# Making the recurrence's elementwise tiles in the projections, in pieces of 128 tokens, with own weight splits and an inverse in two pipeline stages

## The chip, the cores and the metric

The kernel runs on one core of a Trainium2 chip. The metric is the device time of an execution in microseconds; a kernel's time is the median of its timed executions. Engines are named as in the profile; SP here only issues DMAs.

## What is computed

One inference step of a two-layer decoder with 1024 channels, in fp32, for a prompt of 1024 tokens and eight samples of 8 tokens each. Layer 0 mixes by a convolution module, layer 1 by RWKV-7 time mixing; each layer then has cross-attention over 256 memory tokens and an MLP of width 4096. The change lies in layer 1's mixer:

```python
r = xr @ p['rw_w_r'][ri]; k = xk @ p['rw_w_k'][ri]; v = xv @ p['rw_w_v'][ri]
w_pre = p['rw_w0'][ri] + jnp.tanh(xw @ p['rw_w1'][ri]) @ p['rw_w2'][ri]
decay = jnp.exp(-jnp.exp(-jax.nn.softplus(-w_pre) - 0.5))
a = jax.nn.sigmoid(p['rw_a0'][ri] + (xa @ p['rw_a1'][ri]) @ p['rw_a2'][ri])
g = jax.nn.sigmoid(xg @ p['rw_g1'][ri]) @ p['rw_g2'][ri]
kk = k * p['rw_k_k'][ri]                       # then divided by its norm, per head
k = k * (1 + (a - 1) * p['rw_k_a'][ri])
y, s = wkv7_scan(rh, decay, kh, vh, -kk, kk * ah, s0)   # state 64x64 per head, token by token
y = standardize(y, LNX_EPS) * p['rw_lnx_g'][ri] + p['rw_lnx_b'][ri]
bonus = jnp.sum(rh * kh * p['rw_r_k'][ri], axis=-1, keepdims=True) * vh
out = ((y + bonus) * g) @ p['rw_w_o'][ri]
```

## The kernel before

**Two streams.** Stream A carries the first 512 prompt tokens, stream B the other 512 with the 64 sample tokens (576 columns). Each goes through convolution, attention 0, MLP 0, projections, recurrence, output product, attention 1 and MLP 1. The streams are generators; `pace` takes the next step of the one whose summed costs are lower, and a scheduler that works with a simulated timeline then orders each engine's instructions, the recurrence with 1000 instructions of priority. B's recurrence needs A's final state, so it waits for "scan0"; B's MLP 1 runs alone at the end. On-chip memory is given to pools in stacks, A's from the left and B's from the right, and a pool that takes over memory waits for the tiles that held it.

**Split products.** Large products run as three fp32r matmuls on the high and low halves of both operands (`prod`, L142 to L144). `split` makes the halves: ACT copies the high one (L96), DVE subtracts (L97). A weight tile is 128x1024. For the 24 weight tiles of r, k and v, A also writes the low half to DRAM (`put`, tile low) and B loads it from there instead of subtracting.

**Projections** (`projections`). Mixed tokens are made for r, k and v in turn (`mix`), and `project` multiplies them with eight weight tiles, m = 0 to 7, for two token tiles of 256 (A) or 288 (B). Beside the products run sides, one step for each product: `hidden` makes the low-rank inner products (L810), `lora` the outer ones (L856) with Tanh, Sigmoid or a copy behind. Every result goes to DRAM in six slots for each m (scr). The low-rank product for a ran last, after all of `project`.

**Recurrence** (`scan`). A chunk is 64 tokens with all channels, 128 x 512 elements for each quantity; A has 8 chunks, B the samples as one chunk and 8 more. `prep` loads a chunk's r, k, decay input, a and v from scr, makes on DVE, ACT and POOL the key kk, the running sum of the decay (a scan instruction, L1171), its two exponentials, and from them the tiles ar and bk that PE reads, the bonus factor and the head norms; then PE forms the products within the chunk (L1224) and DVE masks them (Aak, Aq). `invert` inverts the chunk's triangular blocks, first in blocks of 16 on DVE, then in blocks of 32 with PE. `rest` does the step on the state (`step`) and `finish` (norm per head, weight, bias, bonus and gate on POOL). `together` interleaves the steps of three chunks: rest of chunk n-2, inverse of n-1, prep of n.

What sets the order around the change: each engine takes its instructions as the scheduler left them, so an instruction that waits holds those behind it; SP does so with the DMAs that it issues.

## Time and profile before

| | us |
| --- | --- |
| median of three timed executions (3832.77 to 3837.16) | 3834.26 |
| the profiled execution | 3837.42 |
| its span, first to last instruction | 3835.7 |
| PE busy in the span (94%) | 3623.9 |
| DVE busy (61%) | 2351.6 |
| ACT busy (42%) | 1610.0 |
| POOL busy (17%) | 660.7 |

How to read it: matmuls are pipelined, so PE's busy time holds work at half clock and waits inside the pipe too; two rows of products at full clock give what one costs.  The first instruction of A's recurrence on PE starts near 1745 us and its last near 2121; B's lie between 2391 and 2862.

### The profile page before, as it was taken

To read this page: it belongs to the slowest core of one execution; us is meant where nothing else is said; L and a number is where in the kernel's file an instruction comes from. 1 tells how busy PE (TensorE), PEld (TensorE's weight loads), DVE (VectorE), ACT (ScalarE), POOL (GpSimd) and SP (SyncE) were. 2 spreads that over 40 slices of the span, in tenths; PEclk is the share of its full clock that TensorE was granted. 3 is DMA by queue.
4 is the path that set the end of the run, shared out by engine and by line. 5 is a ranking of instruction groups with operands and counts; after the bars stand their busy time and mean duration, and the time that the engine had idled before them with its cause. 6 is when DMAs were issued, how large, how long until landed. Compare 5 with 4: busy or idle time off the path is not lost.

```text
span 3835.7 us, 75763 instructions
## 1 busy us (share of the span) xinstructions
PE 3623.9 (94%) x30906; PEld 3369.6 (88%) x30906; DVE 2351.6 (61%) x4479; ACT 1610.0 (42%) x3190; POOL 660.7 (17%) x704
## 2 busy tenths in 40 slices
PE   8989979999999999999979998879999999989998
PEld 7767769999999999998768898758799999989998
DVE  7889974646545554437896444778955546553334
ACT  3223253435433354544555654444543435332222
POOL 0010031114201100002332000243330025101110
PEclk9999989999999999999979998889899999989998
DMA  6414223335422344544333784432233336322222
GB/s 226 132 53 129 80 67 106 102 114 170 153 90 83 126 151 152 159 138 112 85 88 109 232 254 146 111 93 70 54 113 120 114 120 197 121 72 83 83 83 64
DMA packets 333004, 456.03 MB, mean 119 GB/s; under 512 B 155248, under 2 KB 247664, under 8 KB 332656
## 3 DMA queue, kind: packets, MB, share of 16 engines
q1 hardware_dynamic: 305008, 424.43, 36.4%
q10 hardware_dynamic: 27648, 26.75, 2.0%
q8 instruction: 243, 3.98, 0.4%
q14 instruction: 105, 0.86, 0.1%
HBM read 369.11 MB, written 73.49 MB: 115 GB/s over the span
## 4 chain that ended last, share of the span: by engine, by line
PE 77%; DVE 11%; ACT 4%; DMA 4%; issue 2%; POOL 1%; SPq 1%; ACTq 0%; DVEq 0%; POOLq 0%
PE B_d L142 11%; PE B_d L144 11%; PE B_d L143 11%; PE A_d L142 10%; PE A_d L143 9%; PE A_d L144 9%; PE A_d L362 3%; PE B_d L362 2%; DMA scr<-t_st 1%; SPq L1151 1%; PE A_hd L810 1%; PE A_d L442 1%; PE B_sa L608 1%; DVE wt L97 1%; PE B_sa L610 1%
## 5 line engine op out<-in xcount | busy, mean ns | idle before, releaser
L97 DVE TENSOR_TENSOR wt<-raw,wt 128x1024 fp32r<-128x1024 f32 x447 | 567.3, 1272 | 476.9 <-ACT wt L96 473.0
L96 ACT CAST wt<-raw 128x1024 fp32r<-128x1024 f32 x488 | 508.5, 1047 | 502.2 <-PE B_d L144 268.6
L142 PE MATMUL B_d<-hAB,wt 128*128 128x288 f32 (+1 forms) x2240 | 673.6, 303 | 15.4 <-ACT hAB L96 6.3
L143 PE MATMUL B_d<-hBB,wt 128*128 128x288 f32 (+1 forms) x2240 | 668.5, 299 | 1.2 <-DVE hBB L97 1.1
L144 PE MATMUL B_d<-hAB,wt 128*128 128x288 f32 (+1 forms) x2240 | 666.2, 298 | 0.3 <-DVE wt L97 0.3
L142 PE MATMUL A_d<-hAA,wt 128*128 128x256 f32 x2240 | 639.1, 288 | 15.0 <-ACT hAA L96 13.6
L143 PE MATMUL A_d<-hBA,wt 128*128 128x256 f32 x2240 | 642.4, 288 | 3.4 <-DVE hBA L97 3.4
L144 PE MATMUL A_d<-hAA,wt 128*128 128x256 f32 x2240 | 632.8, 285 | 2.5 <-POOL wt L97 2.2
L142 PEld LDWEIGHTS A_d<-hAA,wt 128*128 128x128 f32 x2240 | 429.0, 192 | 25.1 <-ACT hAA L96 16.8
L142 PEld LDWEIGHTS B_d<-hAB,wt 128*128 128x128 f32 x2240 | 425.4, 191 | 24.5 <-ACT hAB L96 7.5
L143 PEld LDWEIGHTS A_d<-hBA,wt 128*128 128x128 f32 x2240 | 430.2, 192 | 14.3 <-DVE hBA L97 5.6
L144 PEld LDWEIGHTS A_d<-hAA,wt 128*128 128x128 f32 x2240 | 428.6, 192 | 7.3 <-POOL wt L97 2.6
L143 PEld LDWEIGHTS B_d<-hBB,wt 128*128 128x128 f32 x2240 | 427.2, 191 | 6.5 <-DVE hBB L97 3.7
L711 POOL TENSOR_TENSOR t_sg<-t_ev 128x256 f32<-128x256 f32 (+1 forms) x256 | 185.5, 725 | 1418.2 <-ACT t_ev L709 1329.3
L144 PEld LDWEIGHTS B_d<-hAB,wt 128*128 128x128 f32 x2240 | 426.1, 190 | 2.3 <-issue 0.7
L142 PE MATMUL B_d<-u,wt 128*128 128x288 f32 x1024 | 307.1, 301 | 0.0
L144 PE MATMUL B_d<-u,wt 128*128 128x288 f32 x1024 | 303.3, 299 | 0.0
L143 PE MATMUL B_d<-u,wt 128*128 128x288 f32 x1024 | 303.3, 298 | 0.0
L143 PE MATMUL A_d<-u,wt 128*128 128x256 f32 x1024 | 288.2, 282 | 0.0
L144 PE MATMUL A_d<-u,wt 128*128 128x256 f32 x1024 | 288.2, 282 | 0.0
L142 PE MATMUL A_d<-u,wt 128*128 128x256 f32 x1024 | 287.4, 282 | 0.0
L97 DVE TENSOR_TENSOR u<-t_sg,u 128x256 fp32r<-128x256 f32 (+1 forms) x256 | 130.4, 510 | 149.9 <-ACT u L96 149.6
(401 smaller groups left out, 7068.8 us busy)
## 6 DMA issues: line engine op xcount, KB each, us to landing
raw<-in_mlp_up_dram SPq DMA_DIRECT2D x128, 512.0 KB, 3.6
raw<-in_mlp_dn_dram SPq DMA_DIRECT2D x128, 512.0 KB, 3.6
raw<-in_rw_w_dram SPq DMA_DIRECT2D x64, 512.0 KB, 4.2
ld<-scr SPq DMA_DIRECT2D x136, 128.0 KB, 3.2
wf<-in_w_in_dram SPq DMA_DIRECT2D x32, 512.0 KB, 4.0
raw<-in_xa_w_q_dram SPq DMA_DIRECT2D x32, 512.0 KB, 3.6
raw<-in_xa_w_o_dram SPq DMA_DIRECT2D x32, 512.0 KB, 3.6
raw<-in_ck_dram SPq DMA_DIRECT2D x32, 512.0 KB, 3.6
```

The lines of the kernel that those rows point to most:

```text
L96: self.nc.scalar.copy(hi, src)
L97: (engine or self.nc.vector).tensor_tensor(lo, src, hi.bitcast(F32), SUB)
L142: self.nc.tensor.matmul(out, lhsT=wh, rhs=mh, start=(i == 0), stop=False)
L143: self.nc.tensor.matmul(out, lhsT=wh, rhs=ml, start=False, stop=False)
L144: self.nc.tensor.matmul(out, lhsT=wl, rhs=mh, start=False, stop=(i == last))
L362: nc.tensor.matmul(ps[:, :n], lhsT=wt[:, 0, k * P:k * P + P], rhs=h[:, k, t0:t0 + n], start=(k == 0), stop=(k == NC8 - 1))
L442: nc.tensor.matmul(ps[hs], lhsT=dg[:, q, h], rhs=two[h][:, 2 * q:2 * q + 512], start=(q == 0), stop=(q == pairs - 1))
L608: nc.tensor.matmul(out[:, h2], lhsT=wt.rearrange("p i t -> p (i t)"), rhs=moving[:, 0], start=start, stop=stop)
L610: nc.tensor.matmul(out[:64, h2], lhsT=wt[:, 0], rhs=moving[:, 1], start=False, stop=False)
L711: nc.gpsimd.tensor_mul(sg[:, :n], r[:, :n], r[:, :n])
L810: nc.tensor.matmul(ps[:, :n], lhsT=w1[:, m:m + P], rhs=hc[:, :n], start=(c == 0), stop=(c == NC8 - 1))
L1151: nc.sync.dma_start(out=dst[..., m * 64:m * 64 + 64], in_=scr[part][m][:, slots, t0:t0 + 64])
```

## The change

**Elementwise tiles.** A new generator `stage(m, c0)` loads the six slots of one m for a piece of 128 tokens (64 for the samples), makes in place r times the decay, kk times the decay, the two tiles of bk, the gated bonus with the bias, and the gate with the weight, and stores the six to a new DRAM tensor, tls. Its tiles kk, t1 and ones (the exponentials) have one buffer, ld has three for A and two for B. There are 32 pieces for A and 40 for B; `project` steps through the pieces of m behind the last product of v for that m. Head norms go to a small tile sums, chunk-end decays to ends. The low-rank product for a becomes a side of `project(2)`, its hidden one of `project(0)`. In the recurrence `prep` loads four of the six slots straight into what PE reads (ld, two buffers), and `finish` loads the other two and runs three POOL instructions where there were five.

**Weight splits.** Both streams split their own weights: `put` and low are gone.

**Inverse.** In two stages: `blocks16` follows `prep` of the same chunk once at is there (`begun`), and `blocks32` runs a round later beside the next chunk's `begun`. dgz and td get two buffers.

```diff
-        if share is not None and self.part:
-            self.nc.scalar.copy(wt[:, 0], raw)
-            self.nc.sync.dma_start(out=wt[:, 1].bitcast(F32), in_=share)
-            return wt
...
-    low = [[dram.tile([P, 1024], F32, name=f"low{i}_{m}") for m in range(NC8)] for i in range(3)]
+
+    tls = [[dram.tile([P, 6, n], F32, name=f"tls{i}_{m}") for m in range(NC8)] for i, (_, n, _) in enumerate(PARTS)]
+
+    sums = [const.tile([P, NC8, n], F32, name=f"sums{i}") for i, n in enumerate((8, 9))]
+    ends = [const.tile([P, NC8, n], F32, name=f"ends{i}") for i, n in enumerate((8, 16))]
...
-        weights = s.weights([(a["rw_w"][i, m], 1024, P, None, None, low[i][m]) for i in range(3) for m in range(NC8)])
...
-        one, lh = (hp.tile([P, np_], F32R, name=f"l{n}") for n in "wh")
+        weights = s.weights([(a["rw_w"][i, m], 1024, P) for i in range(3) for m in range(NC8)])
+
+        lw, la, lh = (hp.tile([P, np_], F32R, name=f"l{n}") for n in "wah")
...
-        hid = {"w": one, "a": one, "h": lh}
+        hid = {"w": lw, "a": la, "h": lh}
...
+        half, pieces = 128, (0, 2, 4, 6, 8)[:4 + part]
+        rst = hp.tile([P, half], F32, name="rst")
+
+        ones = hp.tile([P, half // 64 * 65], F32, name="ones")
+        nc.gpsimd.memset(ones, 1.0)
...
+        less = hp.tile([P, NC8], F32, name="less")
...
+        def stage(m, c0):
+
+            n, l, e, rs, at = (64, DSEQ, tail, tail_rst, slice(8, 16)) if c0 == 8 else (half, 64, ones, rst, slice(c0, c0 + 2))
+            ts = slice(64 * c0, 64 * c0 + n)
+            ld = hp.tile([P, 6, half], F32, tag="ld", name="ld", bufs=3 - part)
+            nc.sync.dma_start(out=ld[:, :, :n], in_=scr[part][m][:, :, ts])
+            w, r, ag, k, v, g = (ld[:, i, :n] for i in range(6))
+            kk, t1 = (hp.tile([P, half], F32, tag=x, name=x)[:, :n] for x in ("kk", "t1"))
+            e = by(e, l + 1)
+            nc.scalar.activation(kk, k, AF.Copy, scale=col("k_k", m))
+            nc.scalar.activation(t1, k, AF.Square, scale=col("k_k", m))
+            ps = s.bank()
+            for i in range(n // 64):
+                for hs in (slice(0, 64), slice(64, P)):
+                    nc.tensor.matmul(ps[hs, i:i + 1], lhsT=t1[hs, 64 * i:64 * i + 64], rhs=bones[hs, hs][:, :1],
+                                     start=True, stop=True)
+            nc.vector.tensor_scalar_max(sums[part][:, m, c0:c0 + n // 64], ps[:, :n // 64], L2_MIN)
+
+            nc.vector.tensor_tensor_scan(out=w, data0=rs, data1=w, initial=0.0, op0=MUL, op1=ADD)
+            nc.scalar.activation(e[:, :, 1:], by(w, l), AF.Exp, scale=-DECAY)
+            nc.scalar.activation(w, w, AF.Exp, scale=DECAY)
+            yield .2
+            nc.scalar.activation(t1, ag, AF.Identity, scale=col("k_a", m), bias=less[:, m:m + 1])
+            nc.vector.scalar_tensor_tensor(out=ag, in0=kk, scalar=-1.0, in1=ag, op0=MUL, op1=MUL)
+            nc.vector.scalar_tensor_tensor(out=t1, in0=t1, scalar=1.0, in1=k, op0=ADD, op1=MUL)
+            nc.gpsimd.tensor_tensor(ag, ag, w, MUL)
+            nc.vector.tensor_tensor(k, t1, w, MUL)
+            nc.vector.scalar_tensor_tensor(out=t1, in0=r, scalar=col("r_k", m), in1=t1, op0=MUL, op1=MUL)
+            nc.gpsimd.tensor_copy(ends[part][:, m, at], e[:, :, l])
+            nc.gpsimd.tensor_tensor(by(r, l), by(r, l), e[:, :, 1:], MUL)
+            nc.vector.tensor_tensor(by(w, l), by(kk, l), e[:, :, :l], MUL)
+            yield .2
+            ps = s.bank()
+            nc.tensor.matmul(ps[:, :n], lhsT=bones, rhs=t1, start=True, stop=True)
+            nc.vector.tensor_tensor(v, v, ps[:, :n], MUL)
+
+            nc.vector.scalar_tensor_tensor(out=v, in0=v, scalar=col("lnx_b", m), in1=g, op0=ADD, op1=MUL)
+            nc.scalar.activation(g, g, AF.Copy, scale=col("lnx_g", m))
+            yield .2
+            nc.sync.dma_start(out=tls[part][m][:, :, ts], in_=ld[:, :, :n])
+
+        def staged():
+
+            for m in range(NC8):
+                yield 0
+                for c0 in pieces:
+                    yield from stage(m, c0)
...
-                        store(t, m, (slot + 1) % 3, t0, n)
+                        store(t, m, (1, 3, 4)[slot], t0, n)
                         yield cost(n)
                         for side in sides:
                             yield next(side, 0)
+                    if slot == 2 and tt == tiles[-1]:
+                        for _ in range(1 + 3 * len(pieces)):
+                            yield next(tiles_of, 0)
                     if m0 == 6 and after is not None:
...
-        yield from project(0, 2, hidden(1, "w", [AF.Tanh]))
-        yield from project(1, 3, hidden(5, "gh", [AF.Sigmoid, AF.Sigmoid]), lora("w", 3))
-        yield from project(2, None, hidden(4, "a", [AF.Copy]), lora("gh", 5))
-        s.put()
-        yield from lora("a", 4)
+        tiles_of = staged()
+        yield from project(0, 2, hidden(1, "w", [AF.Tanh]), hidden(4, "a", [AF.Copy]))
+        yield from project(1, 3, hidden(5, "gh", [AF.Sigmoid, AF.Sigmoid]), lora("w", 0))
+        yield from project(2, None, lora("a", 2), lora("gh", 5))
+        yield from tiles_of
...
-BUF = dict(w=5, bon=2, at=2, ar=2, Aq=2, UV=2, AV=2, BK=2, v=2, pcs=3)
+BUF = dict(w=5, ld=2, at=2, Aq=2, UV=2, AV=2, BK=2, v=2, pcs=3, td=2)
...
-    E65 = filled([P, 8, 65], "E65", 1.0)
-    dg = filled([P, 16, 32], "dgz", 0.0)
+    dgs = [filled([P, 16, 32], f"dgz{i}", 0.0) for i in range(2)]
...
-    def load(dst, c, slots):
+    def load(dst, c, slots, src=tls):
 
         part, t0 = (1, 512) if c is None else (c // 8, c % 8 * 64)
         for m in range(NC8):
-            nc.sync.dma_start(out=dst[..., m * 64:m * 64 + 64], in_=scr[part][m][:, slots, t0:t0 + 64])
-
-    def prep(chunk):
+            nc.sync.dma_start(out=dst[:, m], in_=src[part][m][:, slots, t0:t0 + 64])
...
-        ld = new([P, 4, 512], "ld")
-        load(ld, chunk, slice(1, 5))
...
         v = w512("v")
-        load(v, chunk, 0)
-        ar = new([P, 8, 2, 64], "ar")
-        bk = new([P, 8, 2, 64], "bk")
...
-        kk = w512()
-        nc.vector.tensor_tensor(v3(kk), v3(k), bvec("k_k"), MUL)
-        sq = w512()
-        nc.scalar.activation(sq, kk, AF.Square)
-
-        L = ws
-        nc.vector.tensor_tensor_scan(out=L, data0=masks["rst"], data1=ws, initial=0.0, op0=MUL, op1=ADD)
-        if sam:
-            E = w512()
-            nc.scalar.activation(E, L, AF.Exp, scale=-DECAY)
-        else:
-            E = E65
-            nc.scalar.activation(E[:, :, 1:], v3(L), AF.Exp, scale=-DECAY)
-        En = L
-        nc.scalar.activation(En, L, AF.Exp, scale=DECAY)
-        if sam:
...
-            pcs = new([P, 8], "pcs")
-            nc.gpsimd.tensor_copy(pcs, E[:, :, 64])
-            nc.gpsimd.tensor_tensor(ar[:, :, 0], v3(kk), E[:, :, :64], MUL)
-        t1 = w512()
-        nc.vector.scalar_tensor_tensor(out=v3(t1), in0=v3(ag), scalar=-1.0, in1=bvec("k_a"), op0=ADD, op1=MUL)
-        bp = ag
-        nc.vector.scalar_tensor_tensor(out=bp, in0=kk, scalar=-1.0, in1=ag, op0=MUL, op1=MUL)
-        nc.gpsimd.tensor_tensor(bk[:, :, 0], v3(bp), v3(En), MUL)
-        km = t1
-        nc.vector.scalar_tensor_tensor(out=km, in0=t1, scalar=1.0, in1=k, op0=ADD, op1=MUL)
-        nc.gpsimd.tensor_tensor(ar[:, :, 1], v3(r), v3(E) if sam else E[:, :, 1:], MUL)
-        nc.gpsimd.tensor_tensor(bk[:, :, 1], v3(km), v3(En), MUL)
-        rk = w512()
-        t = w512()
-        nc.gpsimd.tensor_tensor(v3(t), v3(r), bvec("r_k"), MUL)
-        nc.vector.tensor_tensor(rk, t, km, MUL)
+        load(v3(v), chunk, 4, scr)
+        pcs = ends[part][:, :, 8:] if sam else ends[part][:, :, n]
         yield
 
-        ss = bank("pp")
-        for q in range(4):
...
-        for cp, ps in heads:
-            for h, hs in heads:
-                nc.vector.tensor_scalar_max(d4[hs, :, cp], ss[ps, h:8:2].unsqueeze(2).broadcast_to([64, 4, 2]), L2_MIN)
+        d4 = d32[:, :16].rearrange("p (c i) -> p c i", i=2)
+        nc.vector.tensor_copy(d4, sums[part][:, :, n].unsqueeze(2).broadcast_to([P, 8, 2]))
...
+                if (q, h) == (1, 1):
+                    w.update(chunk=chunk, at=at)
+                    yield "at"
+                else:
+                    yield
...
-        sb = bank("pp")
-        nc.tensor.matmul(sb, lhsT=bones, rhs=rk, start=True, stop=True)
-        bon = w512("bon")
-        nc.vector.tensor_tensor(bon, v, sb, MUL)
-        return dict(chunk=chunk, ar=ar, at=at, Aq=Aq, UV=UV, AV=AV, BK=BK, bon=bon, pcs=pcs)
+        w.update(ar=ar, Aq=Aq, UV=UV, AV=AV, BK=BK, pcs=pcs)
 
...
-    def invert(at, tt, deep):
-
-
-
+    def blocks16(w, n):
+
+
+
+        at, deep = w["at"], w["chunk"] is not None
+
+        dg = w["dg"] = dgs[n % 2]
...
-        td = td[:, :8]
+        w["td"] = td[:, :8]
+        yield
+
+    def blocks32(w, n):
+
+        at, td, dg, deep = w["at"], w["td"], w["dg"], w["chunk"] is not None
+        tt = w["tt"] = tts[n % 2]
...
-        gg = w512("gg")
-        load(gg, chunk, 5)
+        gb = new([P, 8, 2, 64], "gb")
+        load(gb, chunk, slice(4, 6))
         nc.gpsimd.tensor_mul(y, y, rs)
-        nc.gpsimd.tensor_tensor(v3(y), v3(y), bvec("lnx_g"), MUL)
-        nc.gpsimd.tensor_tensor(v3(y), v3(y), bvec("lnx_b"), ADD)
-        nc.gpsimd.tensor_add(y, y, w["bon"])
-        nc.gpsimd.tensor_mul(y, y, gg)
+        nc.gpsimd.tensor_mul(v3(y), v3(y), gb[:, :, 1])
+        nc.gpsimd.tensor_add(v3(y), v3(y), gb[:, :, 0])
...
-    def inverse(n, w):
-        w["tt"] = tts[n % 2]
-        yield from invert(w["at"], w["tt"], w["chunk"] is not None)
-        yield
+    def begun(chunk, n):
+
+        w = {}
+        mine, other = prep(chunk, w), iter(())
+        while True:
+            c = next(mine, "end")
+            if c == "end":
+                break
+            if c == "at":
+                other = blocks16(w, n)
+            yield
+            if next(other, "end") != "end":
+                yield
+        for _ in other:
+            yield
+        return w
...
         for chunk in chunks + [None, None]:
-            gens = ([rest(inverted)] if inverted else []) + ([inverse(n, ready)] if ready else [])
+            gens = ([rest(inverted)] if inverted else []) + ([blocks32(ready, n)] if ready else [])
             n += bool(ready)
             if chunk is not None:
-                gens.append(prep(chunk))
+                gens.append(begun(chunk, n))
             w = yield from together(*gens)
```

How the order moves, at three places. A name with p_ in front is a PSUM tile of the recurrence, A_d and B_d are a stream's product banks.

PE, the last low-rank product for a in A's projections, before (lw and w are its operands, hAB, hBB and wt those of a split product of B):

```order
L856 MATMUL A_d<-lw,w_17426 128x256 x2
L143 MATMUL B_d<-hBB,wt 128x288
L144 MATMUL B_d<-hAB,wt 128x288
L142 MATMUL B_d<-hAB,wt 128x288
L143 MATMUL B_d<-hBB,wt 128x288
L144 MATMUL B_d<-hAB,wt 128x288
L142 MATMUL B_d<-hAB,wt 128x288
L143 MATMUL B_d<-hBB,wt 128x288
L144 MATMUL B_d<-hAB,wt 128x288
L856 MATMUL A_d<-lw,w_17426 128x256 x2
L142 MATMUL B_d<-hAB,wt 128x288
```

PE at the end of A's projections, after: the last low-rank products of A, then pieces (t_ and c_bones; L887 the head norms, L906 the bonus), each with its own number of t1:

```order
L843 MATMUL A_d<-la,w_18047 128x256 x2
L843 MATMUL A_d<-lg,w_18059 128x256 x3
L843 MATMUL A_d<-lh,w_18064 128x256
L887 MATMUL A_d<-c_bones,t_18191 64x1 x4
L906 MATMUL A_d<-t_18191,c_bones 128x128
L887 MATMUL A_d<-c_bones,t_18221 64x1 x4
L906 MATMUL A_d<-t_18221,c_bones 128x128
L887 MATMUL A_d<-c_bones,t_18251 64x1 x4
```

Where B's products stood between A's last instructions, 24 rows of twelve pieces now follow each other with nothing between them, and the recurrence's first row comes behind.

DVE, within one round of A's recurrence, before (Aak and Aq are masked products, w, ld, v, bon elementwise tiles of `prep`, M and A of the inverse):

```order
L1229 TENSOR_TENSOR Aq<-p_pp,c_incl_p 128x4x64
L1166 TENSOR_TENSOR w<-ld,vec 128x512
L1171 SCALAR_TENSOR_TENSOR ld<-rst,ld 128x512
L1228 TENSOR_TENSOR Aak<-p_pp,c_strict_p 64x4x64
L1229 TENSOR_TENSOR Aq<-p_pp,c_incl_p 128x4x64
L1192 SCALAR_TENSOR_TENSOR w<-ld,vec 128x512
L1286 STREAM_TRANSPOSE M_19152<-dgz 128x512
L1383 TENSOR_TENSOR Z_19139<-p_pz,AV 128x512
L1194 SCALAR_TENSOR_TENSOR ld<-w,ld 128x512
L1197 SCALAR_TENSOR_TENSOR w<-w,ld 128x512
L1289 TENSOR_SCALAR A_19154<-M_19152,c_sel 128x256
L1290 SCALAR_TENSOR_TENSOR A_19154<-M_19152,c_sel,A_19154 128x256
```

DVE within one round of A's recurrence, after (d is filled from sums; M, T and Y are the inverse in blocks of 16, hc a mixed tile of B's projections):

```order
L1214 COPY d_18652<-sums_105 128x16
L1309 TENSOR_TENSOR M_19419<-A_19318,T_19321 128x64 x2
L770 SCALAR_TENSOR_TENSOR hc<-xB_165,vec,hc 128x288
L1312 TENSOR_REDUCE Y_19420<-M_19419 128x32
L1309 TENSOR_TENSOR M_19419<-T_19321,Y_19420 128x64 x2
L1312 TENSOR_REDUCE T_19321<-M_19419 128x2x4x4
L1309 TENSOR_TENSOR M_19469<-A_19318,T_19321 128x512
L1312 TENSOR_REDUCE Y_19470<-M_19469 128x64
L1309 TENSOR_TENSOR M_19469<-T_19321,Y_19470 128x512
```

The instructions of `prep` on 128x512 (L1166, L1171, L1192, L1194, L1197) have left this place, and a copy of 16 columns (L1214) has come; what they made is made in the pieces.

PE, middle of B's recurrence, before (hAA, hBA and wt are a split product of A):

```order
L1224 MATMUL p_pp<-ar,bk 128x128 x8
L143 MATMUL A_d<-hBA,wt 128x256
L144 MATMUL A_d<-hAA,wt 128x256
L142 MATMUL A_d<-hAA,wt 128x256
L143 MATMUL A_d<-hBA,wt 128x256
L144 MATMUL A_d<-hAA,wt 128x256
L142 MATMUL A_d<-hAA,wt 128x256 x2
L143 MATMUL A_d<-hBA,wt 128x256
L144 MATMUL A_d<-hAA,wt 128x256
L142 MATMUL A_d<-hAA,wt 128x256
L143 MATMUL A_d<-hBA,wt 128x256
L1461 MATMUL p_pz<-rs,c_bones 128x512
```

PE, middle of B's recurrence, after:

```order
L1399 MATMUL p_pz<-Z_31005,tt_27455 64x64 x16
L1407 MATMUL p_half<-ld,S 64x64 x3
L1257 MATMUL p_pp<-UV,Aak 64x64 x16
L1407 MATMUL p_half<-ld,S 64x64 x5
L1411 MATMUL p_half<-Aq,UV 64x64 x8
L1417 MATMUL p_pz<-UV,BK 64x64 x16
L1407 MATMUL p_half<-ld,S 64x64 x8
L1411 MATMUL p_half<-Aq,UV 64x64 x8
L1466 MATMUL p_pz<-y,c_bones 128x512
L1226 MATMUL p_pp<-ld 128x128 x6
L1472 MATMUL p_pz<-rs,c_bones 128x512
```

A's products between the recurrence's rows are gone here: 102 rows with some 1,000 matmuls follow each other in this way.

## Rows read from the trace of the kernel before

**Rows 1.** The page's part 2, PE and granted clock: 40 slices of 95.9 us, tenths.

```profile
PE   8989979999999999999979998879999999989998
...
PEclk9999989999999999999979998889899999989998
```

**Rows 2.** Stretches of the run: us from:to, length, busy (count) by engine, PEclk, DMA, GB/s.

```profile
0.00:1745.00 1745.00, 1668.71 (x11802) 1552.71 (x11803) 1085.49 (x1939) 696.79 (x1419) 233.25 (x284) 0.98 0.40 125
1745.00:2121.00 376.00, 335.76 (x4575) 287.69 (x4574) 308.02 (x688) 203.01 (x410) 114.62 (x103) 0.89 0.36 99
2121.00:2391.00 270.00, 250.34 (x1701) 232.96 (x1700) 111.96 (x247) 141.47 (x303) 9.13 (x14) 0.96 0.69 214
2391.00:2862.00 471.00, 426.08 (x5492) 359.05 (x5491) 366.83 (x751) 224.17 (x448) 161.67 (x126) 0.88 0.30 81
2862.00:3836.00 974.00, 943.01 (x7347) 937.14 (x7345) 479.26 (x856) 344.56 (x614) 142.03 (x179) 0.98 0.34 108
```

**Rows 3.** The same view, two short stretches with one stream's split products only.

```profile
2860.00:2880.00 20.00, 20.00 (x172) 20.00 (x171) 11.30 (x20) 7.95 (x16) 6.01 (x7) 1.00 0.80 265
3600.00:3700.00 100.00, 100.00 (x754) 100.00 (x753) 38.51 (x62) 28.58 (x48) 10.68 (x16) 1.00 0.27 84
```

**Rows 4.** Groups of DVE instructions by line, whole run: xcount | busy us, mean ns | idle before.

```profile
L1171 DVE TENSOR_TENSOR_SCAN ld<-rst,ld 128x512 f32<-128x512 f32 x17 | 26.8, 1578 | 2.2 <-DMA v<-scr 2.2
...
L1192 DVE SCALAR_TENSOR_TENSOR w<-ld,vec 128x512 f32<-128x512 f32 x17 | 17.4, 1026 | 0.0
...
L1197 DVE SCALAR_TENSOR_TENSOR w<-w,ld 128x512 f32<-128x512 f32 x17 | 15.6, 915 | 0.0
L1194 DVE SCALAR_TENSOR_TENSOR ld<-w,ld 128x512 f32<-128x512 f32 x17 | 15.3, 900 | 0.1
...
L1203 DVE TENSOR_TENSOR w<-w 128x512 f32<-128x512 f32 x17 | 13.6, 800 | 0.2 <-PE p_pp L1208 0.2
L1166 DVE TENSOR_TENSOR w<-ld,vec 128x512 f32<-128x512 f32 x17 | 12.5, 733 | 16.8 <-DMA ld<-scr 9.5 <-DMA gg<-scr 3.0 <-DMA v<-scr 2.5
...
L1258 DVE TENSOR_TENSOR bon<-v,p_pp 128x512 f32<-128x512 f32 x17 | 11.5, 679 | 7.8 <-PE p_pp L1256 7.8
...
L1212 DVE TENSOR_SCALAR d<-p_pp 64x8 f32<-64x8 f32 x68 | 11.1, 163 | 3.8 <-PE p_pp L1208 3.0
```

**Rows 5.** Groups of DVE instructions by line, from 1745 to 2121 us.

```profile
L97 DVE TENSOR_TENSOR hBB<-t_dl,hAB 128x288 fp32r<-128x288 f32 x30 | 17.7, 609 | 4.7 <-ACT hAB L96 4.5
L783 DVE SCALAR_TENSOR_TENSOR t_dl<-xB,vec,t_dl 128x288 f32<-128x288 f32 (+1 forms) x32 | 17.2, 544 | 2.2 <-ACT t_dl L782 2.1
...
L97 DVE TENSOR_TENSOR wt<-raw,wt 128x1024 fp32r<-128x1024 f32 x11 | 15.3, 1389 | 3.7 <-ACT wt L96 3.7
L725 DVE TENSOR_TENSOR xB<-xB,B_d 128x288 f32<-128x288 f32 x32 | 14.0, 443 | 1.2 <-PE B_d L144 1.1
...
L738 DVE SCALAR_TENSOR_TENSOR xB<-xB,vec,t_rs 128x288 f32<-128x288 f32 x16 | 12.1, 814 | 0.0
L783 DVE SCALAR_TENSOR_TENSOR hc<-xB,vec,hc 128x288 f32<-128x288 f32 (+1 forms) x18 | 9.7, 538 | 8.0 <-ACT hc L782 7.9
...
L271 DVE TENSOR_TENSOR t_acc<-t_acc,t_sq 128x288 f32<-128x288 f32 x14 | 7.8, 558 | 1.2 <-ACT t_sq L269 1.0
```

**Rows 6.** Groups by line, all engines, whole run, the same columns; then DMA issues.

```profile
L1256 PE MATMUL p_pp<-w,c_bones 128*128 128x512 f32 x34 | 22.8, 757 | 1.4 <-ACT BK L1246 1.4
...
L1463 ACT ACT_TABLE_LOAD x17 | 21.8, 1283 | 0.3
...
L836 ACT CAST w<-raw 128x128 fp32r<-128x128 f32 x64 | 18.6, 293 | 3.5 <-PE B_d L856 2.8 <-PE A_d L856 0.6
...
L841 DVE TENSOR_TENSOR w<-raw,w 128x128 fp32r<-128x128 f32 x48 | 13.9, 292 | 23.5 <-ACT w L836 21.7 <-DMA w<-in_lora_dram 1.4
...
raw<-in_rw_w_dram SPq DMA_DIRECT2D x64, 512.0 KB, 4.2
...
scr<-t_st ACTq DMA_DIRECT2D x96, 144.0 KB, 3.0
```

70 lines of the change are left out of this document (28 added, 42 removed).

## The prediction

> **What bounds the kernel now.** I read the page's slices first, then the stretches. PE is busy nearly everywhere [rows 1], so the time is the work that PE has plus what it loses. The lost part lies where a recurrence runs: in the slices from the nineteenth on PE falls to 7 and 8 tenths and the granted clock leaves full speed [rows 1]. Rows 2 cut the run into five stretches: up to A's recurrence (1745 us), A's recurrence (376), between the two (270), B's recurrence (471), and the rest (974). In the two recurrences DVE is busy 308.02 of 376 us (82%) and 366.83 of 471 us (78%), far above its share elsewhere, and the clock is 0.89 and 0.88 [rows 2]. I take DVE as what paces those two stretches. At full clock one split product costs 100 us / 754 = 0.1326 us for B's 288 columns and 20 us / 172 = 0.1163 us for A's 256 [rows 3]. With these prices the order of the changed kernel says how much product time lies in each stretch; the sum of products is the same in both kernels, 10,176 for each stream.
>
> **Stretch 1, up to A's first piece.** The changed order places 610 B products, 288 A products and 72 small A products (the low-rank ones) behind this point that were ahead of A's recurrence. The slices ahead of the nineteenth are 9 on PE and full on the clock [rows 1], so these left a saturated PE: 610 x 0.1326 + 288 x 0.1163 + 72 x about 0.12 = 123 us. 1745 - 123 = 1622 us. The moved hidden product for a stays within this saturated stretch: its cost was there before, at another place, and I put it at nothing.
>
> **Stretch 2, A's pieces (new).** PE holds 1144 B and 288 A products and the 72 small ones: 151.7 + 33.5 + 8.6 = 194 us. A piece adds PE work of its own: the 128-column product with bones is a quarter of L1256's 22.8 / 17 = 1.34 us [rows 6], and the four one-column ones I bound by the same again, so 0.7 us. While B has products, 20 pieces cost only that, 14 us: their six ACT and nine DVE instructions at 0.293 and 0.292 us [rows 6] are 1.8 and 2.6 us a piece beside some 9 us of products. The last 12 pieces stand on PE with nothing between them (the order shows it), so there the piece loop sets the time. Its bound below is ACT's five instructions up to t1 and DVE's four up to w, one after the other on kk, t1 and ones, which have one buffer: 9 x 0.29 + the small product = 3.2 us. Its bound from the load buffer is a load (4.2 us, by the 512 KB load next in size), the piece (some 5 us) and a store (3.0 us) [rows 6] over three buffers: 4.1 us. I take 4.1, 49 us. 194 + 14 + 49 = 257 us; between 216 (the loop hidden) and 290.
>
> **Stretch 3, A's recurrence.** A chunk loses on DVE L1166, L1171, L1192, L1194, L1197, L1203 and L1258 (6.63 us) and four L1212 of 0.163 against one copy of about 0.2: 7.1 us [rows 4]. Eight chunks give back 57 us. B's share of DVE changes too, counted in the order: 12 more splits of mixed tiles (0.609), 10 more mixings (0.544), 29 more of the hidden kind (0.538) and 5 more weight splits (1.389); 32 additions (0.443), 16 scalings (0.814) and 14 sums of squares (0.558) leave [rows 5]. That is +0.3; some 30 instructions of A's last pieces (0.29), twenty short mixings (about 0.3) and nine lost splits of u (about 0.44) make it +12 us. 308 - 57 + 12 = 263 us. The inverse's second stage now has a round of its own, which shortens the chain of a round but takes no work off DVE, so I keep the share of 82%: 321 us. Bounds: 292 (90%) and 351 (75%). POOL loses seven instructions a chunk, POOL not being what ends the waits; I give nothing for it.
>
> **Stretch 4, B's pieces.** PE holds 1772 A products, 338 B products, some 10 us of memory, attention and norm, 90 small products and 40 pieces: 206 + 45 + 10 + 11 + 28 = 300 us. Of the 270 us of before the same prices explain 214 (703 and 676 products, 172 us, and some 42 us of hidden, low-rank and memory products), so 56 us were lost [rows 2]. DVE gets 40 x 2.6 = 104 us and ACT 40 x 1.8 = 72 us, on engines that were busy 112 and 141 of 270 [rows 2], and the 24 weight splits of B that came from DRAM are now made, 30 us over its projections. I keep the loss at 56: 356 us. The piece loop gives a second bound: with two load buffers 12.2 / 2 = 6.1 us a piece, 244 us, and eight times a product pair with its store, about 75 us: 319 us. So the loop is just hidden; it would rule from about 7 us a piece. Range 318 to 420.
>
> DMAs: each piece loads and stores 384 KB on SP, 144 transfers more in all, against 48 of 512 KB taken away. They stand on SP between B's or A's weight loads, so a store that waits for its piece holds the weights behind it; the next two weights are already in the ring, some 9 us of products.
>
> **Stretch 5, B's recurrence.** DVE gives back 9 x 7.1 = 64 us. Of A's instructions 180 stood here and 98 do now; 82 at the stretch's mean of 366.83 / 751 = 0.49 us [rows 2] are 40 us. 367 - 64 - 40 = 263 us, at 78% 337 us. In the middle the order shows some four rounds of the recurrence without any A product, so DVE has nothing else there and PE waits; that is inside the share. Bounds 292 and 370.
>
> **Stretch 6, the rest.** 2642 A products lay here and 1872 do now: 974 - 770 x 0.1163 = 884 us. B's attention keeps A's products beside it in the order; if A ran out early it would cost some 15 us.
>
> **Sum.** 1622 + 257 + 321 + 356 + 337 + 884 = 3777 us of span against 3835.7. The profiled execution was 3837.42, 1.7 more than its span, and 3.2 above the median of 3834.26; so 3777 + 1.7 - 3.2 = 3776 us.
>
> **Table loads.** The order has 90 table loads on ACT against 56, the new ones where Exp of a piece alternates with Sigmoid of the low-rank product. A load takes 1283 ns, and ACT sat idle 0.3 us in all ahead of 17 of them [rows 6]: 34 x 1.283 = 44 us more on ACT, most of it in stretches 2 and 4. In stretch 4 ACT then carries 141 + 72 + some 26 = 239 of 356 us, two thirds, and DVE 112 + 104 + some 15 = 231, so I put the loads at nothing. The Trainium skill (ScalarE: Activation LUTs, section What ACT_TABLE_LOAD costs) puts a drain of about 1380 ns beside each load, 2.66 us for a switch of set, which would make these 34 some 90 us of ACT, an estimate by that page. The trace shows the load with its 1283 ns and no idle time of that size ahead of it.
>
> **Rivals.** (1) Slower: B's piece loop rules stretch 4. PE takes its instructions in the order given, so a late t1 stops A's products behind it. Each piece hands over some ten times between ACT, PE, DVE and POOL, and each handover can queue behind a weight split of 1.389 us on DVE [rows 5]. From 7 us a piece each further us costs 40 us; from 8.5 us the change loses. At 9 us: 3776 + 80 + 12 x 0.8 for A's tail = 3866 us. For it: one buffer each of kk, t1 and ones. Against it: ACT and DVE are at two thirds there. (2) No change: the round of a recurrence is set by its own chain, not by DVE. The load now fills what the recurrence step reads, in two buffers for three chunks alive, so it starts only when an earlier step has ended. If DVE's share falls to 73%, 263 / 0.73 = 360 us in both: 3776 + 39 + 23 = 3838 us. For it: L1166 waited 16.8 us for loads already [rows 4]. (3) Better: with less on DVE and a shorter inverse the recurrences run DVE at 90%: 292 and 292 us, 3776 - 74 = 3702 us. (4) A change of table holds ACT for twice its load, and nothing hides it: another 34 x 1.283 = 44 us, 3820 us. Against it: the 0.3 us ahead of 17 loads [rows 6]. The rule of the skill named above would do just this.
>
> **How the numbers follow.** Forecast 0.53 (own range 3735 to 3815), rival 1 0.17, rival 2 0.08, rival 3 0.18, rival 4 0.04. The range 3695 to 3860 leaves out most of rival 1 and the lower half of rival 3. A measurement of this kernel tells 0.2%, some 8 us, from no change. Faster: forecast, 3 and 4, 0.75; same: 2, 0.08; slower: 1, 0.17.
>
> **What would show it.** Right: A's recurrence some 55 us and B's some 130 us shorter with DVE at 80% or more in both; a trough on PE of some 50 us ahead of A's recurrence, where only the pieces' lines stand; the stretch ahead of B's recurrence some 85 us longer. Wrong: waits of A's products behind the pieces' products in B's stretch, with pieces 8 us apart or more (rival 1); DVE under 70% in the recurrences with waits for ld (rival 2).

## The result and the profile after

The changed kernel takes 4051.92 us (4 runs, 4049.16 to 4054.84) against 3835.71 of the kernel before measured beside it: 1.0563 times, 95% interval 1.0545 to 1.0581, 216 us slower. The forecast was 3776, with a range up to 3860.

The page's slices of the changed kernel, 101.2 us each, in tenths (as [rows 1]):

```profile
PE   8989979999999999994799888789987899989998
...
PEclk9989989999999999996799988789986899999999
```

There is a hole that the kernel before hasn't: in the nineteenth slice PE falls to 4 and its clock to 6 tenths, at the end of A's pieces. The five slices of 7 and 8 from the twenty-third on are B's pieces; the 270 us at that place ran at a clock of 0.96 before [rows 2].

The same kernel by stretches (columns as in [rows 2]): to A's first piece, A's pieces, A's recurrence, to the end of B's pieces, B's recurrence, the rest:

```profile
0.00:1627.00 1627.00, 1550.54 (x10894) 1433.18 (x10895) 1049.82 (x1886) 655.64 (x1328) 220.82 (x266) 0.98 0.38 117
1627.00:1942.00 315.00, 237.23 (x1804) 224.02 (x1802) 166.17 (x462) 147.91 (x348) 59.12 (x137) 0.85 0.50 151
1942.00:2281.00 339.00, 312.04 (x4440) 263.57 (x4440) 245.63 (x611) 223.12 (x469) 29.86 (x22) 0.92 0.42 110
2281.00:2757.00 476.00, 385.81 (x2727) 354.88 (x2726) 258.32 (x683) 249.45 (x575) 71.63 (x147) 0.85 0.55 169
2757.00:3133.00 376.00, 339.73 (x4885) 281.82 (x4884) 229.07 (x544) 160.90 (x312) 51.80 (x50) 0.86 0.35 89
3133.00:4049.00 916.00, 867.35 (x6680) 859.58 (x6680) 441.38 (x797) 323.73 (x577) 138.16 (x167) 0.97 0.35 108
```

PE is busy 3692.7 us, 69 more than before, and idle some 144 us more; its work hardly differs. Both grow in the same places: where PE waits, its granted clock is lower (0.85 in the stretches with pieces, 0.98 in the first stretch), and what it then does takes longer.

For the comparison I use **lost time**: a stretch's length less the work that PE did in it at full-clock prices. The prices are the spacings of equal instructions in the trace (per form the mean of the shorter three quarters); they give 3247 us of work before and 3255 after.

| stretch | forecast, length | after, length | lost before | lost after |
| --- | --- | --- | --- | --- |
| to A's first piece | 1622 | 1627 | 182 | 175 |
| A's pieces | 257 | 315 | 0 | 111 |
| A's recurrence | 321 | 339 | 131 | 105 |
| to the end of B's pieces | 356 | 476 | 53 | 180 |
| B's recurrence | 337 | 376 | 162 | 144 |
| the rest | 884 | 916 | 61 | 80 |

The pieces lose 238 us more than the same places before, and the recurrences gain 44. Other ways of grouping the instructions shift the levels of lost time by a good deal, but leave these two differences at 230 to 238 and 39 to 47 us.

What PE waited for, by the view of waits (who waited for whom: us, times, longest), first between 1627 and 1942 us, then between 2281 and 2757:

```profile
PE A_d L906 <- DVE t L900: 43.3, 14, 4.1
PE A_d L887 <- ACT t L883: 11.8, 15, 3.4
```

```profile
PE B_d L887 <- ACT t L883: 26.9, 17, 5.2
...
PE B_d L906 <- DVE t L900: 7.2, 8, 2.4
```

L887 and L906 are the pieces' own products, norms and bonus: PE stood 94 us for them in the two stretches, all their rows counted. The other stream's products queue behind them.

The chain of waits through 45 us of B's pieces shows how they follow each other (start, us, what; the first line is the share by line):

```profile
by line: DMA ld<-scr 30.1%; DMA tls<-ld 26.6%; PE A_d L128 4.4%; PE A_d L126 3.9%; PE A_d L127 3.9%; ACT ld L910 3.4%; DVE t_acc L259 3.0%; ACT L892 2.9%; issue 2.6%; ACT wt L95 2.3%; PE B_d L887 2.1%; ACT ones L892 1.8%; ACT t_sq L257 1.6%
...
2435.32 4.91 DMA tls<-ld
2440.25 4.00 DMA ld<-scr
2444.34 0.44 DVE ld L891
...
2446.05 0.21 DVE ld L907
2446.28 0.36 DVE ld L909
2446.67 0.41 ACT ld L910
2447.13 3.16 DMA tls<-ld
2450.31 5.64 DMA ld<-scr
```

A store (4.9 us), then the load into the buffer that it freed (4.0), then the scan L891 of the new piece, which stands on DVE ahead of the bonus product L907 of the piece before, then that piece's store. More than half of this chain is DMA. A piece comes every 11.3 us (451 us for 40, from the first bonus product on), where the forecast had 6.1: between its load and its store a piece of B takes 12.8 us (median), not the "some 5 us" of the forecast. The Trainium skill (DMA: Bandwidth & Descriptors, section Anatomy of one DMA — SWDGE (gpsimd) path) fits 2.0 us and the bytes over 436 GB/s to a transfer, 2.9 us for 384 KB, an estimate by that page and measured on another queue than SP's; the medians here are longer:

```profile
ld<-scr SPq DMA_DIRECT2D x64, 384.0 KB, 3.8
tls<-ld SPq DMA_DIRECT2D x64, 384.0 KB, 3.3
```

### The profile page after: what moved, and what is told of

It reads as the page before. It is cut to its first block, busy times and chain, and to the rows that moved or that the text cites. A ratio compares the mean times of both kernels' runs of the same rounds, so it can differ in the third digit from the quotient of the medians.

```text
span 4048.9 us, 77998 instructions
## 1 busy us (share of the span) xinstructions
PE 3692.7 (91%) x31424; PEld 3417.1 (84%) x31424; DVE 2390.4 (59%) x4981; ACT 1760.7 (43%) x3605; POOL 571.4 (14%) x788
## 4 chain that ended last, share of the span: by engine, by line
PE 68%; DMA 12%; DVE 9%; ACT 7%; issue 3%; SPq 1%; POOL 1%; ACTq 0%; DVEq 0%; POOLq 0%
PE B_d L126 9%; PE B_d L128 9%; PE B_d L127 9%; PE A_d L127 8%; PE A_d L126 8%; PE A_d L128 8%; DMA ld<-scr 4%; DMA tls<-ld 3%; PE A_d L350 3%; PE B_d L350 2%; ACT wt L95 1%; DVE wt L96 1%; DMA scr<-t_st 1%; PE p_pp L1226 1%; SPq L1198 1%
## 5 line engine op out<-in xcount | busy, mean ns | idle before, releaser
L96 DVE TENSOR_TENSOR wt<-raw,wt 128x1024 fp32r<-128x1024 f32 x471 | 591.4, 1258 | 445.0 <-ACT wt L95 443.8
L95 ACT CAST wt<-raw 128x1024 fp32r<-128x1024 f32 x512 | 533.4, 1046 | 509.9 <-PE B_d L128 230.6
```

The lines of the kernel that those rows point to most:

```text
L95: self.nc.scalar.copy(hi, src)
L96: (engine or self.nc.vector).tensor_tensor(lo, src, hi.bitcast(F32), SUB)
```

## The experiments

Each kernel ran on one chip beside the kernel before, which took 3827.87 us (one run) beside the first four kernels and 3831.68 to 3836.74 beside the others. A time without an interval is one run, and differences under 10 us between such times tell little.

### Buffers: does the pace of the pieces cost the time?

e1_ld3: `ld` of B gets three buffers.

```diff
-            ld = hp.tile([P, 6, half], F32, tag="ld", name="ld", bufs=3 - part)
+            ld = hp.tile([P, 6, half], F32, tag="ld", name="ld", bufs=3)
```

> The changed kernel with three load buffers for B's pieces instead of two. In the profile of the changed kernel a piece of B holds its load buffer for a load (4.0 us), the piece (12.5 us) and a store (4.9 us), 21.4 us, so two buffers give 10.7 us a piece; t1, of which there is one, is held for about 8.6 us a piece. Theory 1 (the buffers set the pace, the load buffer first and t1 second): with three buffers t1 is next, 8.6 us a piece, B's piece stretch 350 to 385 us instead of 451, the kernel at 3955 to 3990 us. Theory 2 (ACT and DVE are too busy with the streams' other work, and pieces wait in their queues): nothing moves by more than 20 us, 4030 to 4060 us.

Measured: 4042.89 us, 9 less, and 215 above the kernel before beside it, where the changed kernel has 216: no gain. The stretch itself did about what theory 1 said, 374 us from 476 (348 from 451, counted from the first bonus product on). Stretches of e1_ld3 (B's pieces, B's recurrence, the rest), then PE's waits in the first of them:

```profile
2287.00:2661.00 374.00, 263.65 (x1869) 238.04 (x1867) 186.50 (x526) 190.46 (x447) 53.40 (x132) 0.80 0.60 184
2661.00:3051.00 390.00, 342.83 (x4883) 285.05 (x4884) 265.13 (x631) 186.23 (x381) 56.34 (x48) 0.87 0.36 93
3051.00:4041.00 990.00, 961.75 (x7542) 955.76 (x7541) 483.16 (x868) 354.54 (x630) 152.36 (x185) 0.98 0.34 109
```

```profile
PE B_d L906 <- DVE t L900: 61.6, 21, 4.9
PE B_d L887 <- ACT t L883: 15.3, 23, 2.5
```

The time was not saved but moved: the scheduler now left 101 us of A's products for later, and the rest grew from 916 to 990 us. The stretch loses 173 us where the changed kernel loses 180: PE waits for the pieces 77 us in place of 39, now mostly for the bonus product. **A shorter stretch is no gain if its work only went elsewhere.** My expectation had priced the length, not the loss.

e2_two and e3_ld3_two: two tiles each of kk, t1 and ones; alone, and with e1's buffers.

```diff
-            kk, t1 = (hp.tile([P, half], F32, tag=x, name=x)[:, :n] for x in ("kk", "t1"))
+            kk, t1 = (hp.tile([P, half], F32, tag=x, name=x, bufs=2)[:, :n] for x in ("kk", "t1"))
...
-        ones = hp.tile([P, half // 64 * 65], F32, name="ones")
+        ones = [hp.tile([P, half // 64 * 65], F32, name=f"ones{i}") for i in range(2)]
```

> The changed kernel with two buffers each of kk, t1 and ones (the exponentials), load buffers as they were. Theory 1: the load buffer still gives 10.7 us a piece in B, stretch 430 to 451 us, kernel 4025 to 4055 us; A's tail of pieces, which has three load buffers, may shorten by up to 20 us. Theory 2: nothing moves. A third reading (t1 alone sets the pace): stretch below 380 us, kernel below 3985 us.

> The changed kernel with both: three load buffers for B and two each of kk, t1 and ones. Theory 1: a load buffer gives 21.4 / 3 = 7.1 us a piece and t1 4.3, so PE's own 300 us of work in that stretch is next: stretch 320 to 345 us, kernel 3920 to 3950 us. Theory 2: nothing moves by more than 20 us, 4030 to 4060 us.

Measured: 4054.57 and 4010.42 us. Small tiles alone shorten A's tail of pieces (its recurrence starts at 1916 instead of 1942) and give it all back later. Both together bring 41 us (34, if each is taken against the kernel before beside it), more than theory 2 allowed and well under the 100 of theory 1; B's stretch is 368 us and loses 164. Buffers are a small part of the cause.

### What of a piece costs?

e4_moves_only leaves a piece's arithmetic and products out (its expectation says which), the transfers stay.

```diff
-            nc.scalar.activation(kk, k, AF.Copy, scale=col("k_k", m))
...
-            nc.scalar.activation(g, g, AF.Copy, scale=col("lnx_g", m))
+            nc.vector.tensor_scalar(out=ld[:, :, :n], in0=ld[:, :, :n], scalar1=0.01, scalar2=None, op0=MUL)
```

> The changed kernel whose pieces only load, multiply the six slots by a constant in one DVE instruction, and store: the rest of a piece's arithmetic is left out, on every engine, and the norms and chunk-end decays are constants. All 144 transfers stay where they are. Theory 1 (the pace comes from how long a piece holds its buffers): a buffer is held 10 us, 5 us a piece, PE's work is next: B's piece stretch 300 to 340 us, A's tail of pieces some 30 us shorter, kernel 3880 to 3930 us. Theory 3 (the transfers themselves, on SP's queue and the DMA engines, set the pace): stretch above 420 us, kernel above 4010 us.

Measured: 3849.05 us, 203 less, below even theory 1's range. Its stretches (A's pieces, A's recurrence, to the end of B's pieces, B's recurrence):

```profile
1597.00:1757.00 160.00, 147.85 (x1118) 145.84 (x1116) 64.16 (x122) 52.49 (x117) 13.52 (x22) 0.97 0.90 268
1757.00:2133.00 376.00, 339.01 (x4484) 283.98 (x4482) 250.32 (x612) 191.35 (x388) 38.09 (x45) 0.88 0.35 92
2133.00:2465.00 332.00, 283.63 (x1866) 264.92 (x1864) 154.64 (x317) 148.53 (x313) 8.76 (x12) 0.91 0.79 240
2465.00:2846.00 381.00, 344.36 (x4991) 289.50 (x4990) 261.07 (x622) 192.90 (x392) 58.21 (x47) 0.89 0.36 96
```

The 144 transfers stay, at 0.90 and 0.79 of the DMA engines, and cost little beside the arithmetic: A's pieces lose 20 us instead of 111, B's stretch 93 instead of 180, and a piece of B comes every 5.5 us. Theory 3 falls. B's stretch still loses 40 us more than the same place before (53); whether that is the transfers, the own weight splits or the order is not shown. Note too that this kernel, whose pieces are little more than transfers, is no faster than the kernel before (3827.87 beside it).

e11_no_pe leaves out only what a piece puts on PE.

```diff
-            ps = s.bank()
...
-            nc.vector.tensor_scalar_max(sums[part][:, m, c0:c0 + n // 64], ps[:, :n // 64], L2_MIN)
...
-            nc.tensor.matmul(ps[:, :n], lhsT=bones, rhs=t1, start=True, stop=True)
-            nc.vector.tensor_tensor(v, v, ps[:, :n], MUL)
+            nc.vector.tensor_tensor(v, v, t1, MUL)
```

> The changed kernel whose pieces keep every load, store and all arithmetic on ACT, DVE and POOL, but put nothing on PE: the four one-column products for the head norms and the 128-column product for the bonus are left out (the norms are a constant, the bonus is taken from t1). Theory P (PE takes its instructions in order, so a piece's product that is late stops the other stream's products behind it, and PE's clock falls in these gaps): in the changed kernel PE stood idle 83 us of B's piece stretch and did the rest at a granted clock of 0.85; without the pieces' products the stretch falls from 451 to 320 to 360 us with a clock above 0.93, the kernel to 3900 to 3960 us, not lower since A's tail of pieces stays. Theory Q (the pieces' instructions on ACT and DVE delay the splits of the other stream's products): the stretch stays above 420 us, kernel 4010 to 4060 us.

Measured: 3902.50 us, 149 less, of the 203 that all the arithmetic costs. By the same prices some 30 of the 149 are the products' own time on PE. Its stretches of A's pieces, of B's from the first piece on, and of B's from the end of A's recurrence on (476 us in the changed kernel), then PE's longest waits in the last:

```profile
1627.00:1812.00 185.00, 158.23 (x1133) 151.69 (x1131) 126.13 (x333) 135.53 (x310) 50.29 (x110) 0.96 0.74 219
2247.00:2555.00 308.00, 232.89 (x1448) 213.22 (x1448) 186.04 (x497) 197.16 (x466) 61.24 (x131) 0.84 0.66 202
2150.00:2555.00 405.00, 321.48 (x2066) 296.48 (x2064) 234.45 (x593) 258.61 (x595) 67.45 (x137) 0.87 0.65 201
```

```profile
PE A_d L546 <- DVE e L539: 20.0, 5, 9.9
PE B_d L126 <- ACT t_st L849: 15.7, 10, 2.2
PE A_d L126 <- ACT wt L95: 8.8, 6, 2.9
```

A's pieces lose 40 us instead of 111, at a clock of 0.96. B's stretch was not as theory P said: from the first piece on it is 308 us and still at 0.84, with 75 us of PE idle, now for A's softmax (20), for results that ACT carries off (16) and for weight splits (15). From the end of A's recurrence on PE idles 84 us, against 90 in the changed kernel, and by the same prices the stretch loses only some 30 us less. So theory P holds for A's pieces and the total; in B's stretch taking the products away mostly passed the wait to other lines. Of the 127 us that B's stretch loses more than the same place before (180 against 53), some 30 go with the pieces' products, some 57 more when the rest of their arithmetic goes too (e4_moves_only), and 40 stay. That the 57 come from ACT and DVE handing A's products their operands late, with the pieces among their work (theory Q), fits these waits but is not shown by a run of its own.

e12_skew keeps all work, but writes the products of a piece one piece later, with a tile of its own for the squares and more t1 and load buffers: `first` loads and makes kk, squares and exponentials, `middle` the tiles of ar and bk, `late` has the products, the bonus and the store.

```diff
+                    d = first(m, c0)
...
+                    t1 = middle(*d)
...
+                    if held:
+                        late(*held)
+                    held = (*d, t1)
```

> The changed kernel with the PE products of a piece (norms and bonus) and all that follows them written one piece later, beside the next piece's arithmetic, with a tile of its own for the squares and two (A) or three (B) tiles t1 and four (A) or three (B) load buffers. All work is kept. Theory P (PE stops at a piece's products since they stand in its order before their operands are made): PE's idle time at the pieces' lines falls from 94 us to below 35 us and the kernel to 3910 to 3985 us. Rival: the products are only later, not better placed, or the wait passes to other lines: idle time at the pieces' lines stays above 60 us, or the kernel stays within 30 us of 4010, the kernel with more buffers.

Measured: 3944.44 us, 107 less. Stretches of A's pieces and from A's recurrence to the end of B's pieces, and PE's waits in the second:

```profile
1627.00:1865.00 238.00, 222.97 (x1783) 213.22 (x1781) 143.41 (x404) 137.07 (x330) 54.40 (x125) 0.97 0.65 189
...
2185.00:2572.00 387.00, 290.66 (x2059) 266.82 (x2059) 200.28 (x574) 225.46 (x515) 54.84 (x132) 0.84 0.63 188
```

```profile
PE B_d L909 <- ACT sq L884: 31.1, 13, 11.6
PE B_d L913 <- DVE t L898: 15.6, 11, 2.5
```

In A's pieces PE now waits 11 us for them instead of 55, its clock is 0.97, and 37 us are lost instead of 111; the run's last stretch loses 56 us, where the changed kernel loses 80. At B's pieces it still waits 55 us, mostly for the squares, and PE is still idle 96 us of that stretch. In sum 66 us of idle time at the pieces' lines, not the 35 that I expected but on the rival's side of 60, so my mechanism is right for A and only a part of the story for B. The edit also adds buffers: e3_ld3_two, which has most of them and the old place of the products, is 66 us slower, so some 66 of the 107 us are left for the place and the few further buffers.

### Does DVE set the length of a recurrence?

e13_before_dve2 makes the seven DVE instructions that the change removes twice, in the kernel before.

```diff
+        dum = new([P, 512], "dum")
+        nc.vector.tensor_tensor(v3(dum), v3(k), bvec("k_k"), MUL)
         nc.vector.tensor_tensor(v3(kk), v3(k), bvec("k_k"), MUL)
...
```

> The kernel before with the seven 128x512 DVE instructions of a chunk that the change removes (6.63 us) each made twice, the copy into a tile that nothing reads: 113 us more of DVE over 17 chunks, on the same dependencies. Theory D (DVE's work sets the round of a recurrence, at a share of about 80%): 113 / 0.8 = 141 us more, 3950 to 3985 us. Theory C (the chain of steps sets it, DVE has room): under half of it, 3840 to 3895 us, with DVE's share in the recurrences rising above 85%.

Measured: 3879.23 us, 42 more than before beside it (3836.74), in the range of theory C. DVE is busy 78 us more over the run, not 113. The two recurrences:

```profile
1747.00:2187.00 440.00, 386.92 (x4862) 330.64 (x4860) 357.57 (x780) 231.26 (x472) 112.97 (x103) 0.88 0.38 106
2410.00:2900.00 490.00, 422.04 (x5385) 351.63 (x5383) 399.94 (x803) 215.11 (x433) 146.17 (x118) 0.85 0.28 77
```

They are 64 and 19 us longer at a share of DVE of 81% and 82%, for 83 us more of DVE in the two: in length DVE costs about one for one, near what theory D said, and the share above 85% of theory C did not come. In time it costs half of it: a longer recurrence holds more of the other stream's products (the lost time of the two rises by some 50 us, not 83). Neither theory had it whole.

e6_one_stage takes the inverse back to one stage in the changed kernel (`whole` is blocks16, then blocks32), e7_before_two_stage makes two in the kernel before.

```diff
-            gens = ([rest(inverted)] if inverted else []) + ([blocks32(ready, n)] if ready else [])
+            gens = ([rest(inverted)] if inverted else []) + ([whole(ready, n)] if ready else [])
```

> The changed kernel with the inverse in one stage again, as before the change: blocks of 16 and of 32 of a chunk follow each other in the round after its products. Theory C (a round is as long as its longest chain of dependent steps): A's recurrence goes from 339 to 365 us or more and B's from 376 to 390 or more, the kernel to 4070 to 4110 us. Theory D (DVE's work sets the round): both recurrences stay within 10 us, 4035 to 4065 us.

> The kernel before with only the inverse in two stages (two dgz tiles, one td). Its recurrences keep all elementwise work, DVE at 308 of 376 us and 367 of 471 us. Theory C: the chain of a round is shorter, recurrences 20 to 60 us shorter in sum, 3775 to 3815 us. Theory D: DVE has the same work, 3825 to 3845 us.

Measured: 4030.25 us, 20 less, and 3861.41 us against 3835.64, 1.0067 (1.0048 to 1.0086), 26 more. Theory C had the sign wrong both times, and both times lie outside the range of theory D. Recurrences of e6_one_stage:

```profile
1941.00:2294.00 353.00, 336.94 (x4512) 283.80 (x4512) 243.33 (x621) 228.50 (x487) 27.43 (x23) 0.92 0.42 112
2735.00:3111.00 376.00, 355.80 (x5102) 299.36 (x5100) 244.52 (x578) 172.01 (x341) 59.15 (x58) 0.92 0.36 94
```

PE stands idle 36 us there against 63 in the changed kernel, and the two recurrences lose 229 us against 249; in e7 they lose 317 against 293 before. All parts of the change but the inverse are thus worth 64 us of lost time in the recurrences with one stage (293 to 229) and 68 with two (317 to 249), and two stages take some 20 back. By which step of a round is not shown. What the recurrences gain also hangs on what stands beside them: in e4_moves_only, where they do the same work, they lose at most some 20 us less than in the kernel before.

### The small parts, and whether they add

e8_before_own (own weight splits) and e9_before_lora (the low-rank product for a moved), each alone in the kernel before.

```diff
-        weights = s.weights([(a["rw_w"][i, m], 1024, P, None, None, low[i][m]) for i in range(3) for m in range(NC8)])
+        weights = s.weights([(a["rw_w"][i, m], 1024, P) for i in range(3) for m in range(NC8)])
```

```diff
-        yield from project(0, 2, hidden(1, "w", [AF.Tanh]))
+        yield from project(0, 2, hidden(1, "w", [AF.Tanh]), hidden(4, "a", [AF.Copy]))
...
-        yield from project(2, None, hidden(4, "a", [AF.Copy]), lora("gh", 5))
+        yield from project(2, None, lora("a", 4), lora("gh", 5))
         s.put()
-        yield from lora("a", 4)
```

> The kernel before with only the weight splits changed: B makes the low halves of its 24 weight tiles of r, k and v on DVE (24 times about 1.3 us, 30 us) and does not load them; nothing is written to DRAM for it. B's projections lie in a stretch where DVE is busy 112 of 270 us. Both theories: hidden, within 8 us of before, 3826 to 3844 us; if the splits are late for PE, up to 30 us slower, 3865 us.

> The kernel before with only the low-rank product for a moved: its hidden product beside r's products, its outer product beside v's, own hidden tiles for w and a, three w2 buffers. No pieces, weights shared, inverse in one stage. In the kernel before the last products of a stand at A's end between products of B on a PE that is 9 tenths busy, so every theory has it within 10 us of before, 3825 to 3846 us; more than 15 us either way would make it a part of the loss or gain of its own.

Measured: 3847.80 us, 1.0036 (1.0025 to 1.0047), and 3851.52 us, 1.0045 (1.0029 to 1.0062): 12 and 15 us slower, both beyond the 8 and 10 us in which I expected them. Three small parts, with the two stages, and none is faster.

e14_skew_one_share undoes own splits and two stages in the skewed kernel, e15_skew_one and e16_skew_share one of them each.

> The skewed kernel with two parts of the change undone as well: weight splits of r, k and v shared by way of DRAM again, the inverse in one stage. If the parts add (two stages cost 20 us in the changed kernel and 25 in the kernel before, own splits 12), it is at 3944 - 22 - 12 = 3910 us, between 3895 and 3925. Outside 3885 to 3935 the parts act on each other, and their single prices don't explain the total. Either way it stays slower than the kernel before, since B's pieces keep most of their idle time.

> The skewed kernel (3944 us in one look) with only the inverse back in one stage; own weight splits stay. If the inverse's two stages cost 20 to 25 us here as in the two other kernels: 3915 to 3930 us. If the 18 us that the kernel with both parts undone lost against the skewed one come from the inverse: 3955 us or more.

> The skewed kernel with only the weight splits shared by way of DRAM again; the inverse stays in two stages. If own splits cost 12 us here as in the kernel before: 3925 to 3940 us. If shared splits cost here, since their 48 transfers now stand on SP among the pieces' loads and stores, each of which waits for another: 3955 us or more.

Measured: 3962.07 us (1.0339, 1.0321 to 1.0356), 3939.84 (1.0293, 1.0262 to 1.0324) and 3948.05 (1.0295, 1.0272 to 1.0319). All three lie outside what I expected: the parts don't add. Alone neither moves the skewed kernel's single 3944.44 by more than 5 us; together they make it 18 slower. The prices of 12 to 26 us hold for the order they were measured in: every edit lets the scheduler lay the whole run anew. How the 216 us divide among the small parts therefore stays open; the 203 of the pieces' arithmetic are about ten times as much. No kernel here beats the one before.

## Why the prediction was wrong

**The work was right, the loss was not.** The products counted in the order gave each stretch its work. A's first piece came after 1627 us (forecast 1622), the stretch of B's pieces held 296 us of work (300), and the rest held the 1872 products of A that the order had. The sum failed where it priced what PE loses. (In stretch 3 the terms of B's other DVE work add up to +11, not +12; that moves nothing.)

**B's pieces (120 us of the miss of 272).** The step was "I keep the loss at 56", covered by ACT and DVE at two thirds of the stretch. They were at 249 and 258 of 476 us, even less, and the stretch lost 180 us. Free time on an engine isn't an operand in time: between load and store a piece took 12.8 us where the forecast had some 5, PE was idle 90 us of the 476, and its clock fell to 0.85. Rival 1 named one reason (a late t1 stops A's products behind it) and had the sign. PE did stand 39 us at the pieces' products, but e11_no_pe shows that they are only some 30 of the 127 us lost more than before; the pieces' other arithmetic is some 57, and 40 are left even with transfers alone and stay open. Rival 1's price, 40 us for each microsecond of pace from 7 us on, is refuted: e1 took the pace from 11.3 to 8.8 us and won nothing clear.

**A's pieces (58).** The last twelve, alone on PE, came 5.2 us apart (4.1 forecast); with 5.4 us in which the recurrence then waited for the tiles just stored they took 66 us, not 49. The stretch up to them took 249 us, not 208: "20 pieces cost only that, 14 us" beside B's products put the loss there at nothing. PE waited 11 us at the pieces' lines there; what made up the rest of it isn't shown. e12 shows that most of the 111 us lost in A's pieces could be avoided (37 are left), by the place of the products and by buffers: with two small tiles alone (e2) the stretch is 26 us shorter.

**The recurrences (18 and 39) and the rest (32).** I took DVE as what paces them and kept its share at 82 and 78%. Its work fell further than forecast, to 245.63 and 229.07 us, but the share fell to 72 and 61%: with DVE lighter, something else ends last, and which step is not shown. In e4_moves_only, whose recurrences do the same work, A's is 376 us long as in the kernel before, with DVE at 67%; so even with the pieces' arithmetic left out the time, 3849 us, is 73 over the forecast. e13 shows the size of the error: a microsecond of DVE added to the kernel before is worth about one of a recurrence's length and half of one in time. In B's recurrence I also saw some four rounds without any A product and put them "inside the share". The last 143 us and the start of the rest:

```profile
2990.00:3133.00 143.00, 109.04 (x2113) 84.96 (x2112) 81.93 (x203) 71.26 (x140) 20.29 (x17) 0.74 0.29 64
3133.00:3152.00 19.00, 1.69 (x6) 1.48 (x6) 3.21 (x4) 5.36 (x8) 4.68 (x4) 0.56 0.65 211
```

In the first row PE, at a clock of 0.74, did 57 us of work; in the second, the start of the rest, it waited 18 us for the output product's first operands with nothing of A beside, the "some 15 us" that I had left out of the sum. What made up the other 14 of the rest's 32 us is not shown.

**Table loads (rival 4).** The Trainium skill's 2.66 us for a switch (ScalarE: Activation LUTs, What ACT_TABLE_LOAD costs) do not show as idle time. The 22 loads of 1283 ns ahead of the low-rank results and 12 of the pieces' had 2.0 and 0.2 us of idle time in all before them:

```profile
L849 ACT ACT_TABLE_LOAD x22 | 28.2, 1283 | 2.0 <-ACT t_st L932 1.2 <-ACT ld L893 0.2 <-ACT w L823 0.2
...
L892 ACT ACT_TABLE_LOAD x12 | 15.4, 1283 | 0.2
```

No run here takes the loads alone away, so what they add to a piece's chain is not shown.

**Rivals 2 and 3.** Rival 2's condition came true, DVE's share fell below 73% in both recurrences, but not its reason: e6, with the longer chain of one stage, loses less, and PE waited little for ld there (A's recurrence, then B's):

```profile
PE p_pp L1226 <- DMA ld<-tls: 6.4, 2, 5.4
...
PE p_pp L1226 <- DMA ld<-tls: 2.4, 5, 0.6
```

DVE at 90% (3) was wrong. A chance of 0.17 for slower was too low: the price of a chain on engines that have room was taken as nothing, though the order showed products of a long chain placed between those of a full PE.
